# A batched matmul with its transfers moved between queues: all stores on SyncE, all loads but one on ScalarE, none on GpSimd

## Chip, cores and metric

The kernel runs on one core of a Trainium2 chip. The metric is the device time of one execution in microseconds (us). The kernel before takes 125.35 us, the median of three runs (125.24 to 125.36). The profile is of one execution, and its span, from the first to the last instruction, is 123.5 us. Both inputs and the output lie in the chip's memory (HBM).

A core has five engines, each with its own instruction stream: TensorE (PE in the profile; its weight loads are PEld), VectorE (DVE), ScalarE (ACT), GpSimd (POOL) and SyncE (SP). They run independently and wait for one another on semaphores. A transfer (DMA) is issued by one of them into that engine's queue, and the core's 16 DMA engines then move it.

## What is computed

```python
batch, m, k, n = 16, 512, 512, 512
a: [batch, m, k] float32
b: [batch, n, k] float32
out = np.matmul(a, b.transpose(0, 2, 1)).astype(np.float32)
```

There are 16 products of 512 x 512 matrices, with `b` taken transposed. The inputs have 33.55 MB together, the output 16.78 MB.

## The kernel before

The kernel works through eight pairs of matrices. Of each pair it loads `a` and `b` (2 MB each, 16 KB in one piece for each partition), casts them to bf16 on VectorE, transposes them on TensorE into PSUM, and copies the transposed blocks back to SBUF: those of `a` on ScalarE (`ta`), those of `b` on VectorE (`tb`). TensorE multiplies them into `ps`, and ScalarE copies the products to the output buffer `ob`, from which each of the 16 blocks of 1 MB is stored (8 KB in one piece for each partition).

Loads are numbered n = 0 to 15 (even: `a`, odd: `b`, of pair n // 2) and stores n = 0 to 15. The load buffer `ld` has seven slots, and so has `ob`. Who issues what is laid down by hand:

```python
NL = 7
NO = 7
STORES = "SSSSOSOSOSSOOOOOO"
SW = 5
LATE = {11: (8, 9), 13: (10, 11), 15: (12, 13)}

def load(n, engine=nc.sync):
    ...
    if n >= NL:
        nc.sync.wait_ge(s_cd, n - NL + 2)      # the slot's data has been cast
    engine.dma_start(ld[:, slot], src).then_inc(s_ld[slot], 16)

def landed(n):                                 # semaphore and value at which store n has landed
    ...

def store(n):
    engine = nc.gpsimd if n < STORES.count("S") else nc.sync
    engine.wait_ge(s_out, n + 1)
    engine.dma_start(
        out[n].rearrange("(p j) n -> p j n", j=J), ob[:, n % NO]
    ).then_inc(landed(n)[0], 16)

load(0)
load(1, nc.scalar)
for n in range(2, NL):
    load(n)
for n in range(2 * pairs):                     # SyncE: tell VectorE that load n is there
    nc.sync.wait_ge(s_ld[n % NL], 16 * (n // NL + 1)).then_inc(s_go, 1)
    if n > 0 and n + NL - 1 < 2 * pairs:
        load(n + NL - 1)
    for m in LATE.get(n, ()):
        store(m)
store(batch - 2)

n_st = n_of = 0
nc.gpsimd.wait_ge(s_ld[0], 32)                 # load 7 has landed
for what in STORES:                            # GpSimd: S a store, O an output slot released
    if what == "S":
        store(n_st)
        n_st += 1
    else:
        nc.gpsimd.wait_ge(*landed(n_of)).then_inc(s_of, 1)
        n_of += 1
```

So SyncE issues the loads (load 1 apart) and the stores 8 to 15, and GpSimd issues the stores 0 to 7, the first of them only when load 7 has landed. Stores 8 to 13 are held back by `LATE` until the loads 11, 13 and 15 have landed. In SyncE's queue they also stand behind the loads that were issued ahead of them.

ScalarE runs a loop over the pairs. It waits for a slot of `ob` on `s_of`, which GpSimd raises:

```python
with nc.Fori(0, pairs, engines=[act]) as u:
    for ko in range(KO):
        ...                                    # waits on s_ta
        for e in range(2):
            c = nc.scalar.copy(out=ta[...], in_=tp[...])          # L192
        c.then_inc(s_ea, 1)
    for e in range(2):
        take(s_of, 1)
        dst = ob[:, bass.ds((u * 2 + e) % NO, 1)]...
        for j in range(J):
            ...                                # waits on s_mm
            c = nc.scalar.copy(out=dst[:, j, :]..., in_=ps[:, j, :]...)  # L210
            if e == 0:
                c.then_inc(s_pv, 1)
            elif j in (0, J - 1):
                c.then_inc(s_out, 1)
```

VectorE's and TensorE's loops are the same in both kernels. In VectorE's, L157, L160 and L163 are the casts, L168 and L172 copies within SBUF, L173 the copies of the transposed `b`. In TensorE's, L233 are the transposes and L252 the matmuls. The last store (`batch - 1`, L270) is issued by SyncE in both kernels as soon as ScalarE has made its block.

Of the kernel before, what the change touches and what calls it, by code (L numbers as in the profile page):

```python
# [10 lines left out]
def kernel(  # L11
# [6 lines left out]
    nc = tc.nc  # L18
    P = 128
    batch, M, K = a.shape  # L20
    _, N, _ = b.shape
    J = M // P
    KO = K // P
    HP = P // 2
    HK = K // 2
    pairs = batch // 2
    f32 = mybir.dt.float32
    bf16 = mybir.dt.bfloat16
    NL = 7
    NO = 7  # L30


    STORES = "SSSSOSOSOSSOOOOOO"
    SW = 5

    LATE = {11: (8, 9), 13: (10, 11), 15: (12, 13)}

    def sbuf(name, shape, dtype):
        return ctx.enter_context(nc.sbuf_tensor(name, shape, dtype))

    def sem(name):
        return tc.alloc_semaphore(name)

    with tc.tile_critical(no_gpsimd_drain=True):  # L44
# [8 lines left out]
        ob = sbuf("ob", [P, NO, J, N], f32)  # L53
# [2 lines left out]

        s_set = sem("s_set")
        s_ld = [sem(f"s_ld{i}") for i in range(NL)]
        s_st = [sem(f"s_st{i}") for i in range(SW)]

        s_go = sem("s_go")
        s_of = sem("s_of")
        s_cd = sem("s_cd")
        s_wa = sem("s_wa")
        s_wb = sem("s_wb")
        s_ca = sem("s_ca")
# [2 lines left out]
        s_ta = sem("s_ta")  # L69
# [3 lines left out]
        s_mm = sem("s_mm")  # L73
        s_pv = sem("s_pv")
        s_out = sem("s_out")
# [5 lines left out]
            out=ident[:], in_=ident[:], compare_op=mybir.AluOpType.not_equal, fill=1.0,  # L81
# [3 lines left out]

        def load(n, engine=nc.sync):
            u, slot = n // 2, n % NL
            src = (a if n % 2 == 0 else b)[2 * u:2 * u + 2].rearrange(  # L90
                "e (p j) k -> (e p) j k", j=2 * J
            )
            if n >= NL:

                nc.sync.wait_ge(s_cd, n - NL + 2)
            engine.dma_start(ld[:, slot], src).then_inc(s_ld[slot], 16)

        def landed(n):

            if n < STORES.count("S"):  # L100
                return s_st[n % SW], 16 * (n // SW + 1)

            slot = (n - STORES.count("S") + 2) % NL
            return s_ld[slot], 16 * (len(range(slot, 2 * pairs, NL)) + 1 + (n - STORES.count("S") >= NL))

        def store(n):
            engine = nc.gpsimd if n < STORES.count("S") else nc.sync
            engine.wait_ge(s_out, n + 1)
            engine.dma_start(  # L109
                out[n].rearrange("(p j) n -> p j n", j=J), ob[:, n % NO]  # L110
            ).then_inc(landed(n)[0], 16)

        load(0)
        load(1, nc.scalar)
        for n in range(2, NL):
            load(n)
        for n in range(2 * pairs):
            nc.sync.wait_ge(s_ld[n % NL], 16 * (n // NL + 1)).then_inc(s_go, 1)

            if n > 0 and n + NL - 1 < 2 * pairs:  # L120
                load(n + NL - 1)
            for m in LATE.get(n, ()):
                store(m)
        store(batch - 2)


        n_st = n_of = 0
        nc.gpsimd.wait_ge(s_ld[0], 32)
        for what in STORES:
            if what == "S":  # L130
                store(n_st)
                n_st += 1
            else:
                nc.gpsimd.wait_ge(*landed(n_of)).then_inc(s_of, 1)
                n_of += 1

        def taker(engine):
            return lambda s, n: engine.wait_ge(s, n).then_inc(s, -n)  # L138
# [5 lines left out]
        take = taker(nc.vector)  # L144
# [3 lines left out]
        with nc.Fori(0, pairs, engines=[dve]) as u:  # L148
            for x, (h, w, s_c, s_w) in enumerate(
                ((ha, wa, s_ca, s_wa), (hb, wb, s_cb, s_wb))  # L150
            ):
                src = ld[:, bass.ds((u * 2 + x) % NL, 1)].rearrange("p o j k -> p (o j) k")
                take(s_go, 1)
                if x == 0:
                    take(s_da, 1)

                nc.vector.tensor_copy(  # L157
                    out=h[:, :J, :], in_=src[:, :J, :HK]
                ).then_inc(s_cd, 1)
                nc.vector.tensor_copy(  # L160
                    out=h[:, J:, :], in_=src[:, J:, :HK]
                ).then_inc(s_c, 1)
                nc.vector.tensor_copy(out=w[:], in_=src[:, :, HK:]).then_inc(s_w, 1)  # L163
            for ko in range(KO):
                if ko == 0:
                    take(s_wa, 1)
                    take(s_da, 1)
                    nc.vector.tensor_copy(out=ha[:], in_=wa[:]).then_inc(s_ca, 1)  # L168
                take(s_tb, 1)
                if ko == 1:  # L170
                    take(s_wb, 1)
                    nc.vector.tensor_copy(out=hb[:], in_=wb[:]).then_inc(s_cb, 1)  # L172
                nc.vector.tensor_copy(  # L173
                    out=tb[:, ko, :],
                    in_=tp[:, 2 + ko % 2].rearrange("k j p -> k (j p)"),
                ).then_inc(s_eb, 1)


        act = nc.scalar.engine
        take = taker(nc.scalar)  # L180
        nc.scalar.nop().then_inc(s_ea, 2)
        nc.scalar.nop().then_inc(s_of, NO)
        nc.scalar.copy(out=one[:], in_=nc.const_aps.tensor(1.0, (P, 1), f32))  # L183
        with nc.Fori(0, pairs, engines=[act]) as u:
            for ko in range(KO):

                if ko < KO - 1:
                    nc.scalar.wait_ge(s_ta, ko + 1)
                else:
                    take(s_ta, KO)  # L190
                for e in range(2):
                    c = nc.scalar.copy(  # L192
                        out=ta[:, ko, e * J * P:(e + 1) * J * P].rearrange(
                            "k (j p h) -> k j p h", j=J, h=2
                        ),
                        in_=tp[:, ko % 2, :, e * HP:(e + 1) * HP].rearrange(
                            "k (h j) p -> k j p h", h=2
                        ),
                    )
                c.then_inc(s_ea, 1)  # L200
            for e in range(2):
                take(s_of, 1)
                dst = ob[:, bass.ds((u * 2 + e) % NO, 1)].rearrange("m o j n -> m (o j) n")
                for j in range(J):
                    if j < J - 1:
                        nc.scalar.wait_ge(s_mm, j + 1)
                    else:
                        take(s_mm, J)

                    c = nc.scalar.copy(  # L210
                        out=dst[:, j, :].rearrange("m (p j) -> m p j", j=2 * J),
                        in_=ps[:, j, :].rearrange("m (j p) -> m p j", j=2 * J),
                    )
                    if e == 0:
                        c.then_inc(s_pv, 1)
                    elif j in (0, J - 1):

                        c.then_inc(s_out, 1)


# [1 line left out]
        take = taker(nc.tensor)  # L222
# [43 lines left out]
    with tc.tile_critical(sync_engine=act, no_gpsimd_drain=True):  # L266
        for n in range(batch - NO, batch - 1):
            nc.scalar.wait_ge(*landed(n))
# [40 lines left out]
```

## Time and profile before

| What | Number | View |
|---|---|---|
| time, median of 3 runs | 125.35 us | times |
| span of the profile | 123.5 us | page, heading |
| moved | 50.33 MB, mean 408 GB/s over the span | page, DMA |
| TensorE busy | 91.8 us (74%) | page, part 1 |
| VectorE busy | 68.1 us (55%) | page, part 1 |
| ScalarE busy | 68.1 us (55%) | page, part 1 |
| GpSimd busy | 6.2 us (5%) | page, part 1 |
| mean granted TensorE clock | 0.962 of full speed | cores |
| GpSimd waits for load 7 | 41.3 us, once | waits |
| ScalarE waits for TensorE before the output copies | 25.3 us, 30 times | waits |
| landing of a load, median from its issue | 26.4 us (`a`), 29.9 us (`b`) | page, part 6 |
| landing of a store, median from its issue | 29.2 us (GpSimd), 19.7 us (SyncE) | page, part 6 |

The page divides the span into 40 equal slices of 3.1 us. In a row of slices one digit is the busy share of one engine in one slice, in tenths: 9 is 90% or more. The row DMA is the mean busy share of the 16 DMA engines, and GB/s is what they moved. The part on queues has, for each queue, its number, its kind ("hardware" for SyncE and ScalarE, "software" for GpSimd), its packets, its megabytes and the share of the 16 engines' time that they took.

In a timeline a line has the start in us, the time in us, the engine, the line of the kernel (L210), the operation, what it writes and reads, and how many are merged. In brackets stands the idle time ahead and what ended it. An engine's name with a q (SPq, ACTq) stands for its instruction queue; a DMA's own line covers only its issue, not the transfer. The times of the transfers are in the trace's packet records: each packet has a start, a duration, a size and a queue.

### The profile page before, as it was taken

The page shows a single profiled execution, that of the slowest core. Times are in us where ns is not written, and L with a number is a line of the kernel's source. Part 1 is how long each engine was busy: PE and PEld are TensorE (multiplying, and loading weights), DVE is VectorE, ACT ScalarE, POOL GpSimd, SP SyncE. Part 2 cuts the span into 40 slices and gives each one's busy share as a digit, 9 for nine tenths or more (in the row PEclk, how much of TensorE's full clock was granted, in tenths as well). Part 3 has the DMA queues.
Part 4 walks back from the last instruction along what each step waited for, and adds up shares of the span by engine and source line. Part 5 has one row for each costly group of instructions (what it writes and reads, how often), then busy time and mean ns, then how long its engine had stood idle before and what let it go on. Part 6 is the DMA issues. An engine that isn't in the chain of part 4 may idle for free. (4 is left out here: it accounts for less than half of the span.)

```text
span 123.5 us, 2365 instructions
## 1 busy us (share of the span) xinstructions
PE 91.8 (74%) x768; PEld 57.0 (46%) x768; DVE 68.1 (55%) x96; ACT 68.1 (55%) x130; POOL 6.2 (5%) x14
## 2 busy tenths in 40 slices
PE   0000089999899999989998999899999936999000
PEld 0000079546744774476457547744764435743000
DVE  0000498791898289658938891894788069400000
ACT  4000063458956894596769558947885159465200
POOL 2000000000000070001010150000000000000000
PEclk9999999999999999999999999999999998699955
DMA  4999999999999999999999999999999999999990
GB/s 117 409 425 425 435 441 430 430 425 430 425 430 430 425 430 377 462 401 414 459 401 422 456 403 449 427 414 449 411 425 464 393 430 425 425 427 425 427 401 16
DMA packets 4608, 50.33 MB, mean 408 GB/s; under 512 B 512, under 2 KB 512, under 8 KB 512
## 3 DMA queue, kind: packets, MB, share of 16 engines
q1 hardware_dynamic: 3312, 39.85, 76.1%
q0 software_dynamic: 1152, 8.39, 16.1%
q10 hardware_dynamic: 144, 2.10, 4.4%
HBM read 33.55 MB, written 16.78 MB: 408 GB/s over the span
## 5 line engine op out<-in xcount | busy, mean ns | idle before, releaser
L252 PE MATMUL ps<-tb,ta 128*128 128x512 bf16 x256 | 57.9, 380 | 0.4
L210 ACT COPY ob<-ps 128x512 f32 x64 | 34.5, 588 | 29.3 <-PE ps L252 25.3
L192 ACT COPY ta<-tp 128x512 bf16<-128x512 bf16 x64 | 32.9, 609 | 15.9 <-PE tp L233 15.6
L252 PEld LDWEIGHTS ps<-tb,ta 128*128 128x128 bf16 x256 | 24.3, 98 | 30.5 <-issue 4.0
L233 PE MATMUL tp<-ident,ha 128*128 128x128 bf16 x256 | 20.1, 233 | 19.5 <-PEq L138 19.5
L233 PEld LDWEIGHTS tp<-ident,ha 128*128 128x128 bf16 x256 | 16.9, 104 | 23.3 <-issue 21.5
L173 DVE COPY tb<-tp 128x1024 bf16<-128x1024 bf16 x32 | 21.3, 685 | 5.6 <-DVEq L138 5.6
L233 PE MATMUL tp<-ident,hb 128*128 128x128 bf16 x256 | 18.8, 232 | 2.4 <-PEq L138 2.4
L233 PEld LDWEIGHTS tp<-ident,hb 128*128 128x128 bf16 x256 | 16.8, 105 | 2.8 <-issue 2.8
L157 DVE CAST ha<-ld 128x1024 bf16 x8 | 5.5, 688 | 14.0 <-DVEq L138 13.9
L168 DVE COPY ha<-wa 128x2048 bf16<-128x2048 bf16 x8 | 5.5, 692 | 13.6 <-DVEq L138 13.6
L163 DVE CAST wa<-ld 128x2048 bf16 x8 | 9.8, 1220 | 0.0
L163 DVE CAST wb<-ld 128x2048 bf16 x8 | 9.8, 1219 | 0.0
L157 DVE CAST hb<-ld 128x1024 bf16 x8 | 5.5, 690 | 6.5 <-DVEq L138 6.5
L109 POOL DMA_DIRECT2D out_dram<-ob x8 | 5.5, 697 | 65.5 <-DMA ld<-in_b_dram 41.3
L172 DVE COPY hb<-wb 128x2048 bf16<-128x2048 bf16 x8 | 5.5, 684 | 0.1
L160 DVE CAST hb<-ld 128x1024 bf16 x8 | 5.5, 688 | 0.0
L160 DVE CAST ha<-ld 128x1024 bf16 x8 | 5.5, 686 | 0.0
L183 ACT ACT_TABLE_LOAD x1 | 1.3, 1283 | 1.5 <-SPq L44 1.5
L80 POOL TENSOR_SCALAR_AFFINE_SELECT ident<-ident 128x128 bf16<-128x128 bf16 x1 | 0.3, 283 | 0.2 <-POOL ident L78 0.2
L78 POOL MEMSET ident<- 128x128 bf16 x1 | 0.2, 204 | 0.5 <-SPq L44 0.5
L183 ACT COPY one<-const-float32-1.0 128x1 f32<-128x1 f32 x1 | 0.2, 191 | 0.0
(4 smaller groups left out, 0.4 us busy)
## 6 DMA issues: line engine op xcount, KB each, us to landing
ld<-in_a_dram SPq DMA_DIRECT2D x8, 2048.0 KB, 26.4
ld<-in_b_dram SPq DMA_DIRECT2D x7, 2048.0 KB, 29.9
out_dram<-ob POOLq DMA_DIRECT2D x8, 1024.0 KB, 29.2
out_dram<-ob SPq DMA_DIRECT2D x8, 1024.0 KB, 19.7
ld<-in_b_dram ACTq DMA_DIRECT2D x1, 2048.0 KB, 12.4
```

The lines of the kernel that those rows point to most:

```text
L109: engine.dma_start(out[n].rearrange("(p j) n -> p j n", j=J), ob[:, n % NO]).then_inc(landed(n)[0], 16)
L157: nc.vector.tensor_copy(out=h[:, :J, :], in_=src[:, :J, :HK]).then_inc(s_cd, 1)
L160: nc.vector.tensor_copy(out=h[:, J:, :], in_=src[:, J:, :HK]).then_inc(s_c, 1)
L163: nc.vector.tensor_copy(out=w[:], in_=src[:, :, HK:]).then_inc(s_w, 1)
L168: nc.vector.tensor_copy(out=ha[:], in_=wa[:]).then_inc(s_ca, 1)
L172: nc.vector.tensor_copy(out=hb[:], in_=wb[:]).then_inc(s_cb, 1)
L173: nc.vector.tensor_copy(out=tb[:, ko, :], in_=tp[:, 2 + ko % 2].rearrange("k j p -> k (j p)"),).then_inc(s_eb, 1)
L183: nc.scalar.copy(out=one[:], in_=nc.const_aps.tensor(1.0, (P, 1), f32))
L192: c = nc.scalar.copy(out=ta[:, ko, e * J * P:(e + 1) * J * P].rearrange("k (j p h) -> k j p h", j=J, h=2), in_=tp[:, ko % 2, :, e * HP:(e ...
L210: c = nc.scalar.copy(out=dst[:, j, :].rearrange("m (p j) -> m p j", j=2 * J), in_=ps[:, j, :].rearrange("m (j p) -> m p j", j=2 * J),)
L233: t = nc.tensor.transpose(tp[:, 2 * x + g, j, :], h[:, j, g * P:(g + 1) * P], ident[:])
L252: t = nc.tensor.matmul(ps[:, j, :], ta[:, ko, (e * J + j) * P:(e * J + j + 1) * P], tb[:, ko, :].rearrange("k (j p) -> k j p", j=2 * J)[:, ...
```

## The change

All stores are issued by SyncE, in order, each as soon as its block is made, and the first again only when load 7 has landed. The loads are issued by ScalarE, except load 1, which SyncE issues. GpSimd issues no transfer; it only tells VectorE which loads have landed. The idea is that loads and stores each have a queue of the hardware kind to themselves, and that the order needs no lists laid down by hand.

For this, ScalarE's loop over the pairs is written out, so that it can issue loads and wait on constants. After its copies of a pair's transposes, ScalarE issues the loads 2u + 7 and 2u + 8 into the slots that this pair has left; that order replaces the semaphore `s_cd`. It waits for the landing of store n - 7 itself, in place of `s_of`. `STORES`, `SW` and `LATE` are gone, and each output slot has a semaphore of its own.

```diff
-    STORES = "SSSSOSOSOSSOOOOOO"
-    SW = 5
-    LATE = {11: (8, 9), 13: (10, 11), 15: (12, 13)}
...
-            if n >= NL:
-                nc.sync.wait_ge(s_cd, n - NL + 2)
             engine.dma_start(ld[:, slot], src).then_inc(s_ld[slot], 16)
...
         def landed(n):
+            return s_st[n % NO], 16 * (n // NO + 1)
...
         def store(n):
-            engine = nc.gpsimd if n < STORES.count("S") else nc.sync
-            engine.wait_ge(s_out, n + 1)
-            engine.dma_start(
+            nc.sync.wait_ge(s_out, n + 1)
+            nc.sync.dma_start(
...
-        load(0)
-        load(1, nc.scalar)
+        load(0, nc.scalar)
+        load(1, nc.sync)
         for n in range(2, NL):
-            load(n)
+            load(n, nc.scalar)
         for n in range(2 * pairs):
-            nc.sync.wait_ge(s_ld[n % NL], 16 * (n // NL + 1)).then_inc(s_go, 1)
-            ...                                # loads, late stores, GpSimd's list
+            nc.gpsimd.wait_ge(s_ld[n % NL], 16 * (n // NL + 1)).then_inc(s_go, 1)
+        nc.sync.wait_ge(s_ld[0], 32)
+        for n in range(batch - 1):
+            store(n)
...
-        with nc.Fori(0, pairs, engines=[act]) as u:
+        for u in range(pairs):
             for ko in range(KO):
-                ...
+                nc.scalar.wait_ge(s_ta, KO * u + ko + 1)
                 ...                            # the copies of the transposes
+            for n in (2 * u + NL, 2 * u + NL + 1):
+                if n < 2 * pairs:
+                    load(n, nc.scalar)
             for e in range(2):
-                take(s_of, 1)
+                n = 2 * u + e
+                if n >= NO:
+                    nc.scalar.wait_ge(*landed(n - NO))
                 for j in range(J):
-                    ...
+                    nc.scalar.wait_ge(s_mm, J * n + j + 1)
```

The first cast of each load on VectorE loses its increment of `s_cd`. Work on the data, tiles and bytes moved are the same in both kernels.

More of the change, by code (lines that the diff above doesn't have):

```diff
@@ L58 @@
         s_ld = [sem(f"s_ld{i}") for i in range(NL)]
-        s_st = [sem(f"s_st{i}") for i in range(SW)]
+        s_st = [sem(f"s_st{i}") for i in range(NO)]
         s_go = sem("s_go")
-        s_of = sem("s_of")
-        s_cd = sem("s_cd")
         s_wa = sem("s_wa")
@@ L83, with load @@
         ).then_inc(s_set, 1)
-        def load(n, engine=nc.sync):
+        def load(n, engine):
             u, slot = n // 2, n % NL
@@ L92, in load @@
             )
-            if n >= NL:
-                nc.sync.wait_ge(s_cd, n - NL + 2)
             engine.dma_start(ld[:, slot], src).then_inc(s_ld[slot], 16)
         def landed(n):
[L100 to L104, printed above, removed]
+            return s_st[n % NO], 16 * (n // NO + 1)
         def store(n):
-            engine = nc.gpsimd if n < STORES.count("S") else nc.sync
-            engine.wait_ge(s_out, n + 1)
-            engine.dma_start(
+            nc.sync.wait_ge(s_out, n + 1)
+            nc.sync.dma_start(
                 out[n].rearrange("(p j) n -> p j n", j=J), ob[:, n % NO]
             ).then_inc(landed(n)[0], 16)
-        load(0)
-        load(1, nc.scalar)
+        load(0, nc.scalar)
+        load(1, nc.sync)
         for n in range(2, NL):
-            load(n)
+            load(n, nc.scalar)
         for n in range(2 * pairs):
-            nc.sync.wait_ge(s_ld[n % NL], 16 * (n // NL + 1)).then_inc(s_go, 1)
[L120 to L135, printed above, removed]
+            nc.gpsimd.wait_ge(s_ld[n % NL], 16 * (n // NL + 1)).then_inc(s_go, 1)
+        nc.sync.wait_ge(s_ld[0], 32)
+        for n in range(batch - 1):
+            store(n)
         def taker(engine):
@@ L155 @@
                     take(s_da, 1)
-                nc.vector.tensor_copy(
-                    out=h[:, :J, :], in_=src[:, :J, :HK]
-                ).then_inc(s_cd, 1)
+                nc.vector.tensor_copy(out=h[:, :J, :], in_=src[:, :J, :HK])
                 nc.vector.tensor_copy(
@@ L179 @@
         act = nc.scalar.engine
-        take = taker(nc.scalar)
         nc.scalar.nop().then_inc(s_ea, 2)
-        nc.scalar.nop().then_inc(s_of, NO)
         nc.scalar.copy(out=one[:], in_=nc.const_aps.tensor(1.0, (P, 1), f32))
-        with nc.Fori(0, pairs, engines=[act]) as u:
+        for u in range(pairs):
             for ko in range(KO):
[L187 to L190, printed above, removed]
+                nc.scalar.wait_ge(s_ta, KO * u + ko + 1)
                 for e in range(2):
@@ L200 @@
                 c.then_inc(s_ea, 1)
+            for n in (2 * u + NL, 2 * u + NL + 1):
+                if n < 2 * pairs:
+                    load(n, nc.scalar)
             for e in range(2):
-                take(s_of, 1)
-                dst = ob[:, bass.ds((u * 2 + e) % NO, 1)].rearrange("m o j n -> m (o j) n")
+                n = 2 * u + e
+                if n >= NO:
+                    nc.scalar.wait_ge(*landed(n - NO))
                 for j in range(J):
[L205 to L208, printed above, removed]
+                    nc.scalar.wait_ge(s_mm, J * n + j + 1)
                     c = nc.scalar.copy(
-                        out=dst[:, j, :].rearrange("m (p j) -> m p j", j=2 * J),
+                        out=ob[:, n % NO, j, :].rearrange("m (p j) -> m p j", j=2 * J),
                         in_=ps[:, j, :].rearrange("m (j p) -> m p j", j=2 * J),
```

## The prediction
> **What bounds the kernel now.** I read first the slices of the page, for what stays full over the whole span.
>
> ```profile
> PE   0000089999899999989998999899999936999000
> DVE  0000498791898289658938891894788069400000
> ACT  4000063458956894596769558947885159465200
> DMA  4999999999999999999999999999999999999990
> GB/s 117 409 425 425 435 441 430 430 425 430 425 430 430 425 430 377 462 401 414 459 401 422 456 403 449 427 414 449 411 425 464 393 430 425 425 427 425 427 401 16
> ```
>
> The DMA row is the only one at 9 from the second slice to the last but one, while PE starts at 15 us and ends at 114. So the 16 DMA engines set the time; the compute engines matter only where they fail to hand over work in time. The queues of the page say what is moved:
>
> ```profile
> q1 hardware_dynamic: 3312, 39.85, 76.1%
> q0 software_dynamic: 1152, 8.39, 16.1%
> q10 hardware_dynamic: 144, 2.10, 4.4%
> HBM read 33.55 MB, written 16.78 MB: 408 GB/s over the span
> ```
>
> q1 is SP's queue (15 loads and the last 8 stores), q0 is GpSimd's (stores 0 to 7), q10 is ScalarE's (load 1). A DMA has 144 packets: 128 of data (16 KB each for a load, 8 KB for a store) and 16 small ones. The trace's packet records (start, duration, size, queue) give a median of 611 ns for a 16 KB packet and 309 ns for an 8 KB one. With 8 packets per engine a load takes 8 x 0.611 = 4.89 us and a store 8 x 0.309 = 2.47 us; 16 of each are 117.8 us. In the records data flows from 2.0 to 120.4 us on 15 engines and to 122.0 on one straggler. So there is nearly no gap to win back.
>
> The last pair is where a gap could open. Its lines in the timeline of all engines:
>
> ```profile
> 99.99 0.69 DVE L157 CAST hb<-ld 128x1024 bf16 x1 [4.88 <-DVEq L138]
> 100.15 2.05 ACT L210 COPY ob<-ps 128x512 f32 x4 [4.04 <-ACTq L138]
> ...
> 106.82 7.25 PE L252 MATMUL ps<-tb,ta 128*128 128x512 bf16 x32
> ...
> 113.77 1.09 ACT L210 COPY ob<-ps 128x512 f32 x2 [0.60 <-PE ps L252]
> 115.04 0.33 SPq L270 DMA_DIRECT2D out_dram<-ob  x1
> ```
>
> By the packet records the last load's packets end at 98.85; its first cast is at 99.99, and the last store is issued at 115.04, 16.2 us after the load. That store's packets start at 117.87, right where store 14's end (115.4 + 2.47). So the stores held back have filled this stretch, with 117.87 - 115.04 = 2.8 us between issue and need. The lists `STORES` and `LATE` make that reserve; the change drops them.
>
> **What the Trainium skill says.** "DMA: Bandwidth & Descriptors", section "Queues, rings and completion order", says that each DMA engine takes turns between the queues that have work, a packet at a time. The trace agrees: from 47.3 us on, while q0 holds stores and q1 loads, q0's stores start at 47.3, 54.8, 62.1, 69.4, 76.7, 84.1, 91.4, thus 7.3 to 7.5 us apart, and 8 x (0.611 + 0.309) = 7.36 us is one load packet in turn with one store packet. Stores get a third of the bytes, not half. The same page, section "Issuing engines are not separate DMA queues", says that issuing from more engines saves only the issue time; the slices above agree, for they stay about 425 GB/s with one queue busy (20 to 45 us) and with two (50 to 97). Its "Specifications" give first-byte latency as about 0.6 us from SP or ScalarE and 1 us from GpSimd. The trace shows more: ScalarE's load issued at 0.91 has its first packet at 1.95, SP's issued at 0.95 at 2.87, GpSimd's first store issued at 43.01 only at 47.3. The measured 1.0, 1.9 and 4.3 us are used here. "Runtime: NRT & Kernel Launch", section "Instruction fetch mechanics", says that straight code is fetched ahead in blocks of 256 instructions at little cost. No stretch of before tests that, since its loops are short.
>
> **The change part by part.**
>
> *Bytes and packets.* Unchanged: 16 loads of 128 packets of 16 KB, 16 stores of 128 packets of 8 KB, so 117.8 us of DMA work. Neither queue is faster. First loads: load 0 now on ScalarE's queue and load 1 on SP's, the mirror image; the two share until about 12.3 us as now.
>
> *Loads issued by ScalarE.* Now loads 7 and 8 go out after pair 0's copies of the transposes, 9 and 10 after pair 1's, and so on. These lines of ScalarE's timeline date it:
>
> ```profile
> 20.67 2.05 ACT L192 COPY ta<-tp 128x512 bf16<-128x512 bf16 x4 [2.03 <-PE tp L233]
> ...
> 30.41 4.11 ACT L192 COPY ta<-tp 128x512 bf16<-128x512 bf16 x8
> 35.81 1.07 ACT L210 COPY ob<-ps 128x512 f32 x2 [1.29 <-PE ps L252]
> ```
>
> So 7 and 8 are issued near 22.8, 9 and 10 near 34.5, and with the 11.5 us of a pair, 11 and 12 near 46, 13 and 14 near 57.5, load 15 near 69. In the records of before the DMA engines reach load 7 at 36.6, 9 at 46.5, 11 at 61.5, 13 at 76.2, 15 at 90.8. Every load is in its queue over 12 us early: no gap. On ScalarE a load costs 0.33 us of issue (the SP rows of the timeline after the first six); two are 0.66 us, inside the 1.29 us in which ScalarE waits for TensorE anyway. The first six take some 3 us before its first copy at 16.6.
>
> *The written-out loop.* Drops the eight address computations of a pair and the loop's branch; ScalarE is busy 68.1 of 123.5 us, so this is worth nothing off the bound.
>
> *Stores from SP.* Store 0 still waits for load 7, at 43.0. With 1.0 to 1.9 us of latency in place of 4.3 its packets start near 44.5, 2.8 us earlier. That isn't free: in shared time a load needs 7.36 us, alone 4.89, so 2.8 us more of sharing push the last load back by 2.8 x (7.36/4.89 - 1) = 1.4 us, to about 100.2. All 16 stores go in order from one queue, and sharing lasts to the end of the loads as now, since 7 or 8 stores are let through by then and TensorE has made store 7's data by about 64.
>
> *Slots of the output.* Seven, as before. Block n waits until store n - 7 has landed. From 44.5 in steps of 7.36, store 0 lands near 52, store 1 near 60, store 3 near 75, store 6 near 97; ScalarE's copies of blocks 7, 8, 10 and 13 are at 62, 70, 82 and 97 in before without the wait. Only block 13 is close, and there before waits until 100.15 (the 4.04 us above); this eases by some 3 us.
>
> *The end.* By the last load's end, about 100.2, sharing has moved (100.2 - 44.5) / 7.36 = 7.6 stores; the other 8.4 take 8.4 x 2.47 = 20.7 us, to 121 as now. The last store is issued near 115.04 + 1.4 - 0.3 = 116.1, where 0.3 us is my estimate of what the eased block 13 gives (TensorE's wait of 0.34 us for ScalarE at 104.31). Its packets are ready at 117.1 to 118.0, and wanted at 117.87. So the reserve shrinks from 2.8 us to about 1.8, just about the latency: a gap of 0 to 0.2 us.
>
> *Sum.* 125.35 + 0.1 for the gap, minus up to 0.4 us should slow load packets vanish (some 50 of them, 640 to 890 ns, between 45 and 60 us, as GpSimd's stores set in: 50 x 0.13 / 16 = 0.4), plus about 0.3 for a colder TensorE, below: about **125.4 us**.
>
> **The rivals.**
>
> (a) *The tail opens.* If the stores got half of the bytes, each would go out as soon as it is made, about 12 of them before the last load and not 7.6. That load would end near 2 + 16 x 4.89 + 12 x 2.47 = 110, and with the 16.2 us to the last issue, and the 125.35 - 117.87 = 7.5 us after its packets start, the time would be 133, 6% more. Against it: the 7.36 us spacing, measured on just such packet sizes. A smaller form is real: the windows show 0.83 of the clock in 100 to 110 us and the records half clock from 103.8 to 107.2, after TensorE's waits for load 15. If that load is 1.4 us later, these waits grow, and half clock may last another such stretch of 3.4 us, costing up to 1.7 us: 127 us.
>
> (b) *Loads starve*, because ScalarE issues them late or its queue blocks on a slot. It would show as slices below 9 between 35 and 90 us. The 12 us of lead speak against it; lost time would be a few us.
>
> (c) *Stores fall in behind the loads* if the two queues of the hardware kind don't take turns. The first two loads of before did (q1 and q10 both moved about 210 GB/s from 3 to 12 us). Even in order of issue the engines stay full: again 125.
>
> (d) *GpSimd's part was a cost of its own*: its slow start, its slow packets, the straggler. Without it up to 1.5 us might come back: 124. The straggler is already some 1.5 us behind at 5 us, long before GpSimd's first store, which speaks against most of it.
>
> **Range and chances.** The bytes fix the centre; (a) in its small form pulls up to 127, (d) down to 124, so 124.5 to 126.7 holds it 8 times in 10. Faster by 2% would need 122.8, below the packets' own 117.8 us plus start and end: 1%. Slower by 2% needs 127.9, the tail opened by over 2.5 us: 5%.
>
> **What would show it.** DMA at 9 in all slices but the first and last; the q10 row with 15 loads and no q0 row; stores' first issue near 43 on SP; loads ending near 100; ScalarE's wait before block 13 short; the last store issued near 116 and its landing near 122. Wrong would be a dip in the DMA row near 116 to 118 (tail) or in mid-kernel (starved loads), or a granted clock well below 0.96.

## The result and the profile after

The changed kernel takes **125.09 us** (median of 4 runs, 124.88 to 125.43) against 125.29 us of the kernel before in the same comparison. The ratio is 0.9989, with a 95% interval of 0.9969 to 1.0009: no difference that can be told from zero. The prediction was 125.4 us, within 124.5 to 126.7.

The page's slices of the kernel after, in the same order as before, with the granted clock added:

```profile
PE   0000089999999899989998999999699936997000
PEclk9999999999999999999999999999999999999965
DMA  4999999999999998999999999999999999999991
GB/s 144 394 426 431 447 437 431 426 431 426 426 431 426 426 405 373 453 399 437 407 429 426 463 405 442 437 415 434 423 418 458 399 426 423 431 429 423 426 431 45
```

The DMA row is full again, with no dip near 116 to 118 us (the slices 38 and 39) and none in mid-kernel but the 8 at 46 to 49 us, where the stores set in. The same place has 377 GB/s before and 373 after.

The page's queues (queue, kind, packets, MB, share of the engines' time) show that the transfers did move:

```profile
q10 hardware_dynamic: 2160, 31.46, 60.6%
q1 hardware_dynamic: 2448, 18.88, 36.4%
q14 instruction: 2, 0.01, 0.0%
```

ScalarE's queue carries 15 loads, SyncE's one load and 16 stores; GpSimd's is gone. One instruction fetch of 8 KB, at 48.8 us, stands in the records of after and not of before; it took 508 ns of a DMA engine, and no wait is put down to it. ScalarE's program, written out, is the one that got longer; whose fetch it is isn't recorded.

ScalarE's timeline shows where it issues loads 9 and 10, and SyncE's timeline shows the stores:

```profile
32.29 0.33 ACTq L87 DMA_DIRECT2D ld<-in_b_dram  x1
32.66 0.45 ACTq L87 DMA_DIRECT2D ld<-in_a_dram  x1
34.75 1.07 ACT L177 COPY ob<-ps 128x512 f32<-128x512 f32 x2 [1.11 <-PE ps L218]
...
42.75 69.25 SPq L94 DMA_DIRECT2D out_dram<-ob  x15
113.98 0.33 SPq L236 DMA_DIRECT2D out_dram<-ob  x1
```

Before, GpSimd's timeline had the first stores here:

```profile
43.01 2.39 POOL L109 DMA_DIRECT2D out_dram<-ob  x4 [41.33 <-DMA ld<-in_b_dram]
```

ScalarE's two issues lie ahead of a copy that waits 1.11 us for TensorE in any case. Store 0 is issued at 42.75 (43.01 before), and by the packet records its packets start at 46.6 (47.3 before). The last load ends at 99.4 (98.85), and the last store is issued at 113.98 (115.04).

The end, in the timeline of all engines:

```profile
98.80 2.05 ACT L177 COPY ob<-ps 128x512 f32<-128x512 f32 x4 [3.07 <-DMA out_dram<-ob]
...
100.41 0.69 DVE L130 CAST hb<-ld 128x1024 bf16 x1 [4.77 <-DVEq L111]
...
102.00 1.05 PE L199 MATMUL tp<-ident,hb 128*128 128x128 bf16 x16 [2.61 <-PEq L111]
...
104.94 1.06 PE L199 MATMUL tp<-ident,hb 128*128 128x128 bf16 x16
105.83 7.29 PE L218 MATMUL ps<-tb,ta 128*128 128x512 bf16 x32
```

The wait for a slot ahead of block 13 is there again, 3.07 us against 4.04, now put down to the store's landing itself. VectorE gets load 15 0.4 us later than before, yet the matmuls start 1.0 us earlier. Most of that is the granted clock, full here and half from 103.8 to 107.2 before. The same transposes in the timeline of before:

```profile
101.58 1.05 PE L233 MATMUL tp<-ident,hb 128*128 128x128 bf16 x16 [1.91 <-PEq L138]
...
105.12 1.91 PE L233 MATMUL tp<-ident,hb 128*128 128x128 bf16 x16
```

The last 16 took 1.06 us, against 1.91. This belongs to the two profiled executions and not to the change: the mean granted clock is 0.958 to 0.980 over the four executions of the changed kernel and 0.953 to 0.980 over those of the kernel before. None of this moves the end: the last store's packets start at 117.90, against 117.87 before, when store 14 has gone out.

### The profile page after: what moved, and what is told of

Same layout as the page of the kernel before. It is cut to its first block, busy times and chain, and to the rows that moved or that the text cites. A ratio compares the mean times of both kernels' runs of the same rounds, so it can differ in the third digit from the quotient of the medians.

```text
span 123.1 us, 2235 instructions
## 1 busy us (share of the span) xinstructions
PE 90.1 (73%) x768; PEld 54.7 (44%) x768; DVE 67.9 (55%) x96; ACT 67.9 (55%) x130; POOL 0.7 (1%) x6
## 5 line engine op out<-in xcount | busy, mean ns | idle before, releaser
L177 ACT COPY ob<-ps 128x512 f32<-128x512 f32 x64 | 34.3, 590 | 26.3 <-PE ps L218 22.5
L199 PE MATMUL tp<-ident,ha 128*128 128x128 bf16 x256 | 18.5, 224 | 18.8 <-PEq L111 18.3
L199 PEld LDWEIGHTS tp<-ident,ha 128*128 128x128 bf16 x256 | 15.8, 100 | 22.3 <-issue 20.6
L199 PE MATMUL tp<-ident,hb 128*128 128x128 bf16 x256 | 17.5, 223 | 3.8 <-PEq L111 3.5
L199 PEld LDWEIGHTS tp<-ident,hb 128*128 128x128 bf16 x256 | 15.3, 100 | 5.0 <-issue 4.8
```

Of the source, the lines that this page charges most:

```text
L177: c = nc.scalar.copy(out=ob[:, n % NO, j, :].rearrange("m (p j) -> m p j", j=2 * J), in_=ps[:, j, :].rearrange("m (j p) -> m p j", j=2 * J),)
L199: t = nc.tensor.transpose(tp[:, 2 * x + g, j, :], h[:, j, g * P:(g + 1) * P], ident[:])
```

## The experiments

The ratios are to the kernel before, with 95% intervals. Every edit is made to the changed kernel. Times of packets are from the packet records.

### Is it the transfers alone? Only the transfers left

```diff
-        (all of VectorE's, TensorE's and ScalarE's computation, and its waits)
+        nc.gpsimd.memset(ob[:], 0.0).then_inc(s_set, 1)
+        # load n >= 7 waits for the landing of load n - 7; store 0 for load 7
```

> The computation is left out: only the 16 loads and 16 stores remain, in the same shapes and queues as the changed kernel, the first store again after load 7, nothing waiting for data. Theory (the DMA engines' packets set the time, and neither the queues nor the computation add to it): 125.0 us, within 124.6 to 125.4, data packets from about 2 to 120.4 us on most engines. Rival (the computation, or its tail, still costs something beside the transfers): 123.5 us or less. If the one straggling engine comes from ScalarE's table load, which is absent here, the last packets end near 120.5 and not 121.6, and the time is about 1 us less.

Measured: 124.09 us, ratio 0.9925 (0.9906 to 0.9944). This kernel computes nothing and stores zeros. So 99% of the time is there without any computation, and the theory misses by 1.0 us. The records show what the 1.0 us is: the last packets end at 120.72, and after 80 us no store packet takes over 309 ns. In the changed kernel 32 of them take over 317 ns, up to 361, most of them one after another on a single engine; one engine ends at 121.6, one at 121.2, the others near 120.5. The straggler comes with the computation, or with the table load.

### Which part of the computation makes the straggler? Three runs beside the bare transfers

The table load is put back:

```diff
+            if n == NL:
+                nc.scalar.copy(out=one[:], in_=nc.const_aps.tensor(1.0, (P, 1), f32))
```

> The transfers alone, as in floor, plus ScalarE's table load and its one-element copy after the first six loads are issued. Theory (the table load's own transfer holds up one of the DMA engines early on and leaves the straggler that the kernel before and the changed kernel have): the last packets end near 121.6 on one engine and near 120.5 on the others, time 125.0 us. Rival (the straggler comes from the computation's traffic or from somewhere else): last packets end near 120.7 and the time is 124.1 us, as in floor.

Measured: 124.14 us, ratio 0.9928 (0.9913 to 0.9942), last packets at 120.78. The table load isn't it.

VectorE runs free on constant data:

```diff
+        with nc.Fori(0, 9, engines=[dve]):
+            for h in (ha, wa, hb, wb) * 3:
+                nc.vector.tensor_copy(out=h..., in_=ta[:, 0:2]...)   # 128x2048 bf16
```

> The transfers alone, as in floor, beside VectorE running free on 108 bf16 copies of 128x2048 in SBUF (results unused, nothing else computed). If VectorE's traffic in SBUF slows the one straggling DMA engine: packets over 309 ns, last packets near 121.6 on one engine, 125.0 us. If not: 124.1 us as in floor, last packets near 120.7.

Measured: 124.11 us, ratio 0.9928 (0.9904 to 0.9951), last packets at 120.81. VectorE's copies aren't it.

TensorE runs free on constant data:

```diff
+        with nc.Fori(0, 9, engines=[pe]):
+            # 64 matmuls of 128x128 from ident, then 32 of 128x512 from ta, into ps
```

> The transfers alone, as in floor, beside TensorE running free on constant data (9 rounds of 64 matmuls of 128x128 and 32 of 128x512, results unused, nothing else computed). If TensorE's work or its instructions slow the one straggling DMA engine: packets over 309 ns after 80 us, last packets near 121.6 on one engine, 125.0 us. If not: 124.1 us as in floor, last packets near 120.7.

Measured: 125.08 us, ratio 0.9990 (0.9978 to 1.0002), 33 store packets over 317 ns after 80 us, last packets at 122.0. The rows of TensorE and of the DMA engines in its page:

```profile
PE   0499989998999899979998999899989998999300
DMA  4999999999999999999999999999999999999991
```

TensorE alone beside the transfers brings back the whole microsecond, although no transfer waits for it. Store packets over 317 ns after 80 us number 39, 32 and 33 where TensorE works (before, after and here), and 0, 2 and 6 in the three runs without it. In the changed kernel 29 of the 32 lie between 98.9 and 114.2 us, and TensorE's last matmul ends at 113.1.

In this run's trace two engines end at 122.0, and they fell back in two ways. One did at once: a transfer lands on the 16 DMA engines one by one, and the last of them was 0.5 us behind the median at load 9 (55.9 us) and 1.4 us at load 10 (64.1 us). Between the two lies an instruction fetch of 16 KB, which took 931 ns of a DMA engine at 58.0 us. The other fell back packet by packet, in the slow store packets. The records of before have no such fetch, and its straggler ends at 122.0 as well. Whether the matmuls, their weight loads or the instruction stream slow the packets was not tried.

So 125.1 us is what these bytes take in these packets and this order beside a working TensorE. The kernel before and the changed kernel both stand on that floor, which leaves a new assignment of the queues nothing to gain.

### Does the issuing engine matter? Stores back on GpSimd

```diff
-            nc.sync.wait_ge(s_out, n + 1)
-            nc.sync.dma_start(
+            nc.gpsimd.wait_ge(s_out, n + 1)
+            nc.gpsimd.dma_start(
...
-            nc.gpsimd.wait_ge(s_ld[n % NL], 16 * (n // NL + 1)).then_inc(s_go, 1)
-        nc.sync.wait_ge(s_ld[0], 32)
+            nc.sync.wait_ge(s_ld[n % NL], 16 * (n // NL + 1)).then_inc(s_go, 1)
+        nc.gpsimd.wait_ge(s_ld[0], 32)
```

> The changed kernel with the fifteen stores issued by GpSimd in place of SyncE, and SyncE in place of GpSimd telling VectorE what has landed: the queue part of the change undone, its order kept. Theory (the queue that issues makes no difference while packets take turns): 125.1 us, within 124.8 to 125.5, store 0's packets about 4 us after its issue. Rival (transfers issued by GpSimd cost DMA time or delay): 125.6 us or more, with q0 packets slower than 309 ns or a larger straggler.

Measured: 125.15 us, ratio 1.0004 (0.9994 to 1.0014). GpSimd's timeline has the first stores here:

```profile
43.18 2.25 POOL L94 DMA_DIRECT2D out_dram<-ob  x4 [41.50 <-DMA ld<-in_b_dram]
```

Their packets start at 47.1, 3.9 us after the issue; SyncE's took 46.64 - 42.75 = 3.9 us as well. GpSimd's stores have packets of 309 ns and the same straggler (121.5). The rival is out: with the order kept, it makes no difference here whether the stores have the software or a hardware queue.

### Is the order still needed? Store 0 without its wait for load 7

```diff
-        nc.sync.wait_ge(s_ld[0], 32)
```

> The changed kernel without the wait for load 7 ahead of store 0. Theory (stores let through early push the last load back and use up the reserve of stores that covers the last pair): store 0 is issued near 27.4, its packets start near 31.3, the last load ends near 105.5 (99.4 now), the last store is issued near 120.2, while the stores ahead of it end near 118; its packets then start near 122 and the time is 129.4 us, within 128.5 to 130.5. Rival (the bytes alone set it, any order keeps the engines full): 125.1 us.

Measured: 129.29 us, ratio 1.0363 (1.0315 to 1.0412). The four executions took 128.15 to 130.25 us; the ratio leaves out the slowest, over 1.5% above the fastest, and the profile is of the fastest. The DMA rows of its page, then the stores in SyncE's timeline:

```profile
DMA  4999999999999999999999999999999999996195
GB/s 130 405 436 415 446 436 425 431 420 363 405 451 407 425 423 425 446 415 451 410 441 415 438 428 425 444 410 451 410 446 418 444 425 415 425 420 254 42 415 208
...
27.70 91.64 SPq L94 DMA_DIRECT2D out_dram<-ob  x15
121.33 0.33 SPq L235 DMA_DIRECT2D out_dram<-ob  x1
```

The slices 37 and 38 hold 254 and 42 GB/s: the engines run dry. The last load ends at 106.6 (expected 105.5), and the last store is issued at 121.33 (120.2). Stores let through 15 us too early cost some 4 us at the end, while every byte is the same. The one wait for load 7 is the piece of the old hand-made order that still does the work; `LATE` wasn't needed.

### More reserve still? Store 0 waits for load 9

```diff
-        nc.sync.wait_ge(s_ld[0], 32)
+        nc.sync.wait_ge(s_ld[2], 32)
```

> The changed kernel with store 0 waiting for load 9 in place of load 7. Theory (seven output slots: holding stores back longer ends the loads earlier but lets ScalarE run out of slots): store 0's packets start near 56 and it lands near 64, block 7 is wanted at 61; blocks 9 to 11 wait for stores 2 to 4, block 11's copies start near 93.6 (84.2 now), and two pairs of 11.5 us later the last store is issued near 119.5; 126.7 us, within 126.0 to 127.5. Rival (only the reserve at the end matters, and more of it is better or harmless): 125.1 us or less.

Measured: 126.39 us, ratio 1.0089 (1.0049 to 1.0129). A line of its waits (engine, line, waited for: us in total, times, longest), one of ScalarE's timeline and one of SyncE's:

```profile
ACT ob L177 <- DMA out_dram<-ob: 12.9, 4, 4.6
...
93.29 2.05 ACT L177 COPY ob<-ps 128x512 f32<-128x512 f32 x4 [3.18 <-DMA out_dram<-ob]
...
119.70 0.33 SPq L236 DMA_DIRECT2D out_dram<-ob  x1
```

In the changed kernel this wait is 3.8 us, twice. Here ScalarE runs out of slots four times, block 11's copies start at 93.29 (93.6 expected), and the last store is issued at 119.70 (119.5). Load 7 lies between two losses: two loads later costs slots, no wait costs the tail. Load 8 was not tried.

### How do queues share? Loads in packets of 8 KB

```diff
-            engine.dma_start(ld[:, slot], src).then_inc(s_ld[slot], 16)
+            for h in range(2):
+                engine.dma_start(
+                    ld[:, slot, h * J:(h + 1) * J], src[:, h * J:(h + 1) * J]
+                ).then_inc(s_ld[slot], 16)
...                                            # whoever waits for a load counts 32 in place of 16
```

> Each load is issued as two DMAs with 8 KB a packet in place of one with 16 KB; bytes and order unchanged. Theory (queues take turns packet by packet): load and store packets are now equal, stores get half of the bytes while both are queued, one store every 4.9 us; they catch up with production, the last load ends near 110, and the time is 134 us, within 131 to 136. Rival (queues share by bytes or in another ratio, or packets of half the size cost nothing): stores stay 7.4 us apart and the time stays 125.1 to 126 us. On the 3.9 us from store 0's issue to its first packet: if it is load packets that the DMA engines already hold, it falls to about 2 us; if it is a fixed delay of the issue, it stays 3.9.

Measured: 133.69 us, ratio 1.0681 (1.0656 to 1.0706). From 46.9 us the stores start every 4.9 us (46.9, 51.8, 56.7, 61.6), not every 7.4. The last load ends at 112.6 (about 110 expected). The slices of its page:

```profile
PE   0000389998999999891399999899505999679920
DMA  4999999999999999999999999999999997950095
```

The last but three and the last but two are empty: all loads and all finished stores are out, and the last pair is still computed. Both spacings are what turns packet by packet give, 8 x (0.611 + 0.309) = 7.36 us and 8 x (0.309 + 0.309) = 4.94 us. So these queues share by packets, and the 2:1 of the sizes 16 KB and 8 KB lets one store through with each load, which is just the number of blocks that a load stands for. On store 0's delay, it was issued at 43.20, so the delay is 3.7 us. Load packets of half the size didn't halve it, so it isn't a fixed number of packets that the engines hold; what it is stays open.

### How large is the reserve? The last block made late

```diff
+                    if n == batch - 1 and j == J - 1:
+                        for x in range(8):
+                            nc.scalar.copy(out=ta[...], in_=ps[:, j, :])
```

> The changed kernel with eight more ScalarE copies (128x512, about 0.59 us each, 4.7 us in all, into a part of ta that is no longer read) ahead of the last copy of the last block. Theory (a reserve of 117.9 - 114.0 us, less some 2 us from issue to first packet, so 2 us, hides a late last store): 125.1 + 4.7 - 2 = 127.8 us. Rival (the 3.9 us between issue and first packet seen at store 0 apply here as well, so there is no reserve): 129.8 us. Rival (the last store isn't on the path): 125.1 us.

Measured: 125.75 us, ratio 1.0055 (1.0022 to 1.0087), nine executions from 125.14 to 126.70: less than any theory had but the last, and above that one. The end in its timeline:

```profile
113.90 4.02 ACT L179 CAST ta<-ps 128x512 bf16<-128x512 f32 x8
117.72 0.69 ACT L180 COPY ob<-ps 128x512 f32<-128x512 f32 x1
118.59 0.33 SPq L239 DMA_DIRECT2D out_dram<-ob  x1
```

The eight copies took 4.0 us and not 4.7, for each took 0.50 us. The last store's packets start at 119.42, only 0.83 us after the issue, on idle DMA engines: store 14's packets had ended at about 118.0 on all but the straggler. In that pause of 1.4 us the straggler catches up: the last packets end at 122.1 on all engines, 0.5 us after the 121.6 of the changed kernel.

How long before 117.9 must the last store be issued, while store 14's packets still fill the engines? The two runs above show it: without the wait and with load 9, it was issued at 121.33 and 119.70, and its packets start 1.05 and 1.04 us later, right behind store 14's. With 0.8 to 1.05 us, the reserve in the profile of the changed kernel is 117.9 - 113.98 - 1.05 or 0.83, thus 2.9 to 3.1 us. In the profile of this run the last block was 0.6 us later even without the eight copies, and the reserve 2.3 to 2.6 us. So the 3 us is good to about half a microsecond from one execution to the next. The 3.9 us of store 0 don't apply here.

### One queue for all

```diff
-            nc.sync.dma_start(             # stores
+            nc.scalar.dma_start(
+            if u == 2: (wait for load 7, then stores 0 to 3, ahead of loads 11 and 12)
+            if u >= 2: (stores 2u and 2u + 1 after the pair's output copies)
```

> All loads but load 1 and all stores but the last are issued by ScalarE into one queue, so that each store stands behind the loads issued ahead of it: the rival of order of issue, made real. Theory (full engines set the time, the way in which queues share matters only for the last load's end): stores and loads in blocks in place of turns, the last load ends near 100, and the time is 125.1 us, within 124.8 to 126.0. Rival (two queues of their own are needed): over 127 us, with ScalarE waiting for slots.

Measured: 126.80 us, ratio 1.0153 (1.0112 to 1.0194). Neither side's number: worse than 125.1, better than 127. ScalarE never waits for a slot. The page's GB/s row and a line of ScalarE's timeline:

```profile
GB/s 142 394 452 425 420 436 431 425 431 425 446 425 425 425 425 441 417 347 357 425 433 444 378 436 415 428 449 420 425 415 436 441 404 428 428 428 425 155 420 210
...
56.51 3.06 ACTq L87 DMA_DIRECT2D ld<-in_a_dram  x1
```

There are two slices of about 350 GB/s as the first stores come through (53 to 59 us), and one issue that held ScalarE for 3.06 us where others take 0.33 to 0.54. The last load ends at 103.4, the last store is issued at 118.27, and the engines run nearly dry for some 2 us (the slice of 155 GB/s). So this order of issue doesn't ruin the kernel, but two queues that take turns do better; other orders in one queue were not tried. Why the slices dip, and why the one issue took so long, is open.

### Two attempts to beat both kernels

The table load first, and loads 0 to 6 from SyncE:

```diff
-        load(0, nc.scalar)
-        load(1, nc.sync)
+        nc.scalar.copy(out=one[:], in_=nc.const_aps.tensor(1.0, (P, 1), f32))
-        for n in range(2, NL):
-            load(n, nc.scalar)
+        for n in range(NL):
+            load(n, nc.sync)
...
-        nc.scalar.copy(out=one[:], in_=nc.const_aps.tensor(1.0, (P, 1), f32))
```

> The changed kernel with the table load as ScalarE's first instruction and the loads 0 to 6 all issued by SyncE, so that the table load has ended before ScalarE's first transfer and starts before any data packet flows. If the straggling engine comes from the table load meeting the data packets, it is gone, the last packets end near 120.7 and the time is 124.3 us, less some 0.3 us more at the start, as data flows from 2.7 and not 1.9. If the straggler has another cause: 125.1 to 125.6 us.

Measured: 125.36 us, ratio 1.0021 (1.0012 to 1.0030), straggler at 122.0. The edit moved more than the table load. A line of SyncE's timeline:

```profile
33.12 80.84 SPq L94 DMA_DIRECT2D out_dram<-ob  x15
```

Load 7 is now the first in ScalarE's queue, lands at 33.1, and lets store 0 be issued at 33.12. Its packets start only at 51.64, behind the loads of its own queue, of which the last starts at 41.87. That is 5.0 us later than in the changed kernel, and still the last store's packets start at 117.92, as they do there.

The last store cut into 120 and 8 rows:

```diff
-    last = nc.sync.dma_start(out[batch - 1]..., ob[:, (batch - 1) % NO])
+    last = nc.sync.dma_start(out[batch - 1]...[:120], ob[:120, (batch - 1) % NO])
+    nc.sync.dma_start(out[batch - 1]...[120:], ob[120:, (batch - 1) % NO])
```

> The changed kernel with the last store cut into 120 rows and 8 rows; by the Trainium skill's page on DMA a transfer of 120 rows uses the lowest 15 of the 16 DMA engines and one of 8 rows the lowest 8, so that engine 15 gets nothing of the last store. If the straggler is engine 15, its 1.2 us of delay are hidden: last packets end near 120.8 and the time is 124.3 us. If it is another engine, it gets a row more or as many as now: 125.1 to 125.6 us.

Measured: 125.44 us, ratio 1.0036 (1.0022 to 1.0051), one engine ends at 122.4, and 13 packets of the two parts took 380 to 742 ns, where the changed kernel has none over 361. If rows go to the engines as the Trainium skill's "DMA: Bandwidth & Descriptors", section "Why a DMA increments its semaphore by 16 and not by 1", has it, the straggler is not engine 15; no run here names the engine of a packet. It fits that nine packets of 309 ns follow one another up to 122.4, eight for the engine's share of the 120 rows and one of the 8. The same page's section "Latency and other measured facts" calls engines 7 and 15 usually slower and suspects the descriptors of GpSimd's transfers. Here a straggler stays without any transfer from GpSimd (121.6 us after, 122.0 before), so that cause doesn't fit this one.

## Why the prediction was right, step by step

**Bytes and packets: right.** The floor runs show it directly: 125.08 us with transfers and TensorE alone.

**Turns packet by packet: right.** With loads in packets of 8 KB the stores got half of the bytes, and the time was 133.69 us. That is rival (a) made real, whose terms add up to 133.6 (the text has 133).

**ScalarE's loads: right.** Issued two or more us earlier than estimated (20.6, 32.3, 43.8, 55.2, 66.7), ahead of a wait for TensorE of 1.1 us; no slice is starved. Rival (b) is out.

**Stores from SyncE: the term that was mis-sized.** The prediction took 1.0 to 1.9 us from issue to first packet, read from the idle start of the kernel, and set it against GpSimd's 4.3 us, read beside full engines. So it got a start near 44.5; it was 3.9 us and 46.6. For store 0, beside engines full of loads, SyncE and GpSimd needed 3.7 to 4.3 us alike. So the 2.8 us of earlier sharing were 0.7, and the last load moved by 0.5 us and not by 1.4.

**The end: wrong in its sign.** The reserve was to shrink: the last store issued near 116.1, 1.8 us before 117.87, where before had 2.8 us, and a gap of 0 to 0.2 us. It grew instead: the issue came at 113.98, 3.9 us before its packets started at 117.90. The last load was late by 0.5 us and not by 1.4, and the clock stayed full. The latter is luck of the profiled execution. The prediction's reason for a colder TensorE, longer waits for load 15, doesn't hold either: TensorE waited 2.61 us until 102.0 and kept the full clock, where before it waited 1.91 us until 101.6 and had half the clock from 103.8. And the latency that the reserve has to cover is 0.8 to 1.05 us here, not up to 1.9, so some 3 us stay over.

**Slots: right**, with block 13's wait shorter by 1 us and not 3, again because store 0 started later than thought.

**The 0.4 us of slow packets: wrong.** They come with the first stores, whoever issues them. Between 42 and 62 us, 54 load packets take 640 ns or more after, against 48 before and 51 with GpSimd's stores in the changed order. Nothing was won there, and rival (d) falls with it. The straggler, its other part, comes with TensorE's work. The prediction read it as 1.5 us behind at 5 us. The landings don't show that: in before the last of the 16 engines is 0.5 us behind the median from the first load to load 7 (42.7 us), as it is in the run of the transfers alone, 1.1 us at load 15 and 1.8 us at the last store.

**Rival (c)** is out for the change itself, as the two queues take turns. Its second half, that order of issue gives 125 as well, failed in the one order tried: 126.80 us.

The errors cancelled or lay inside the reserve, and that is why the total held: with the DMA engines of this kernel full from 2 to 120 us, a shift of a microsecond in a wait is absorbed until it uses up the 3 us at the end. The terms for the gap, the slow packets and the clock (+0.1, up to -0.4, +0.3) all failed to come, and as they nearly cancel in the sum, the 125.4 us didn't suffer. That part is luck.

## What to carry to other kernels

When the DMA row is full from end to end, ask only two things of a change in the queues: does work ever run out, and is enough of it left to cover the computation after the last load? When stores start, and how large their packets are beside those of the loads, answers both here (3 to 4% and 6.8% for getting them wrong). Whether GpSimd or SyncE issues the stores answers neither, as long as loads and stores keep queues of their own; both in one queue cost 1.5% in the order tried. Before looking for more, run the transfers alone, and then beside the busiest engine: the floor tells when to stop.

## What was not expected of the hardware

- From issue to first packet store 0 took 3.7 to 4.3 us beside another queue's loads, for SyncE and GpSimd alike, and for load packets of 16 KB and of 8 KB. The last store took 0.83 us with idle DMA engines, and 1.04 and 1.05 us right behind the store ahead of it in its own queue, with the engines full. So full engines alone don't make the 4 us.
- TensorE working on constants, with no transfer waiting for it, lengthened a kernel of transfers from 124.09 to 125.08 us: 8 KB packets then took up to 352 ns in place of 309, and one engine lost 0.9 us about the time of an instruction fetch. VectorE's copies left it at 124.11 us.
- When the stores started beside the loads, about 50 load packets took 640 to 1,100 ns in place of 611, which is 0.4 to 0.6 us of all engines' time, and one slice fell to about 375 GB/s.
